# The third stage's order with a price on each change between gate products and RWKV's products, a shorter chunk pace, and a lower mark for gate products put in ahead

## The chip, the cores and the metric

The kernel runs on one core of one Trainium2 chip. The metric is the device time of one execution in microseconds (us); a lower time is better. One execution of the kernel before was profiled, and all rows below come from it. Names of engines are those of the profile: PE is TensorE (PEld its weight loads), DVE VectorE, ACT ScalarE, POOL GpSimd, SP the engine that issues the DMA transfers.

## What is computed

A trunk of two layers is applied to two sequences (1024 and 2048 tokens, width 1024). The first layer has an S5 mixer and a bidirectional RWKV-7 mixer, each multiplied by its own SiLU gate; the second is windowed attention. Cut to what matters for the change:

```
def s5_branch(u, z, p):
    ...
    y = jax.nn.gelu(y)
    y = y * jax.nn.sigmoid(y @ p['s5_glu_w'].astype(F32) + p['s5_glu_b'].astype(F32))
    return y * jax.nn.silu(z.astype(F32))

def rwkv_scan(r, w, k, v, kk, b, reverse):
    ...
    def step(S, inp):
        r_t, w_t, k_t, v_t, kk_t, b_t = inp
        sa = -jnp.einsum('bhvk,bhk->bhv', S, kk_t)
        S = (S * w_t[:, :, None, :] + sa[..., None] * b_t[:, :, None, :]
             + v_t[..., None] * k_t[:, :, None, :])
        return S, jnp.einsum('bhvk,bhk->bhv', S, r_t)
```

The RWKV state S goes through every token, once forward and once backward. The gates z and the S5 branch's GLU are plain matrix products with no order among the tokens.

## The kernel before

The kernel has four stages. The third (`mixers`) does two things at once on one core: RWKV's scan (`rwkv`), which is a long chain of small steps, and the gate work (`gates`), which is large and free of order. It takes the stretch from about 1114 to 2268 us of the profiled span.

**RWKV.** Tokens are cut into tiles of 128 and these into 4 chunks of 32. For each tile and direction: the decays (L1096, a scan on DVE at L1113), scaled keys on POOL (L1150, L1165), the inner products of a chunk (L1186 and L1187, masked on DVE at L1206), turned keys (L1196, copied by ACT at L1215), and for each window of four tiles the inverses of 32x32 triangular systems, 60 small DVE operations (L1251, L1253) between transposes. Then comes the chain proper, for each chunk: PE L1311, ACT L1314, PE L1320, ACT L1325, PE L1333 and L1334, DVE L1340, and the next chunk of that direction; the outputs (PE L1356, ACT L1363) hang off it. Both directions run side by side; there are 96 pairs of chunks (32 of the first sequence, 64 of the second).

**Gates.** 1536 products of 128x128 by 128x128 (L887, each two instructions in the trace) make z for both branches. When they are done, their weight tile `w` is used again for the GLU: 12 units of 256 tokens, each a load of S5's outputs, a gelu (ACT L932, DVE L934 and L936, ACT L938, DVE L940), 16 products of 128x256 (L970), and four times ACT L950, DVE L955 and a store. Two units' gelus are held at once (`act_at`), and two tiles of z (`zp`).

**What sets the order.** A planner (`Plan`) runs the tasks of both parts on a model of the engines, with a cost for each, and writes every engine's instructions in the order of the model's starts. On the chip each engine goes through its list in that order. Three numbers touch PE's list. A gate product has the last rank (`RF` is 9), so that it gets PE where it can start before the best RWKV task and end within `SLACK` of that start, and also ahead of an RWKV task that could start as early, where the columns of the model's last PE tasks would stay under `NEED`. `PACE` is the shortest distance in the model from one chunk of a direction to its next, in hundredths of a microsecond.

Of the kernel before, what the change touches and what calls it, by code (L numbers as in the profile page):

```python
# [34 lines left out]
class Event:  # L35


    def __init__(self, need=1, t=0.0):
        self.need, self.at = need, t
# [46 lines left out]
class Plan:  # L86
# [3 lines left out]


    SLACK = 0.25
    NEED = 3800
    ISSUE = 0.48
    AFTER = {"PE": 0.28, "SP": 0.0, "ACT": 0.1, "DVE": 0.14, "POOL": 0.1, None: 0.0}

    def __init__(self):
        self.clock = dict.fromkeys(self.AFTER, 0.0)
        self.queue = 0.0
        self.recent = deque()  # L100
        self.tasks = []
        self.now = 0.0

# [11 lines left out]
    def run(self):  # L115
        while self.tasks:
            best = {}
            for task in sorted(self.tasks, key=lambda x: x[0]):
                eng, cost, *waits = task[2]
                ts = [w if isinstance(w, float) else w.t for w in waits]  # L120
                if None in ts:
                    continue
                if eng == "SP":
                    n, cost = cost
                start = max(ts + [self.clock[eng] if eng else 0.0])
                if eng == "PE":
                    cost, cols = cost
                    if task[0] == 9 and eng in best and start <= best[eng][0] + 0.02:
                        end = start + best[eng][1]
                        if sum(c for t, c in self.recent if t > end - 3.413) + best[eng][2][2][1][1] < self.NEED:  # L130
                            best[eng] = start, cost, task
                            continue
                if eng not in best or (start < best[eng][0] and start + cost < best[eng][0] + self.SLACK):
                    best[eng] = start, cost, task
            assert best, "the plan is stuck"
            start, cost, task = min(best.values(), key=lambda x: x[0])
            eng = task[2][0]
            self.now = start
            if eng == "SP":
                n, cost = task[2][1]  # L140
                self.clock[eng] = start + self.ISSUE * n
                self.queue = max(self.queue + cost, start + self.ISSUE * n + 0.65 + cost / n)
                self.advance(task, self.queue + 1.1)
            else:
                if eng:
                    self.clock[eng] = start + cost
                if eng == "PE":
                    while self.recent and self.recent[0][0] < start - 4:
                        self.recent.popleft()
                    self.recent.append((start + cost, task[2][1][1]))  # L150
                self.advance(task, start + cost + self.AFTER[eng])

# [117 lines left out]
class Program:  # L270
# [5 lines left out]
    BACK = 2.0  # L276
    AFTER = {"PE": 0.2, "ACT": 0.14, "DVE": 0.13, "POOL": 0.08, "SP": 0.0}
    BEFORE = {"PE": 0.1, "ACT": 0.0, "DVE": 0.0, "POOL": 0.03, "SP": 0.1}
# [135 lines left out]
    def put(self):  # L414
# [17 lines left out]
        while done < len(ops):  # L432
# [27 lines left out]
            for j in after[i]:  # L460
                f = ops[j][0]
                early[j] = max(early[j], end + (0.0 if e == f == "PE" else self.AFTER[e] + self.BEFORE[f]))
                left[j] -= 1
# [7 lines left out]
class Kern:  # L471
# [3 lines left out]
    WIN = 2  # L475
    RM, RD, RC, RI = 2, 1, 1, 4
    GH = 2
    PACE, RF = 900, 9
    PACE2, LEFT = 600, 0
    GV = 2  # L480
    WR = "x", "mix"
# [545 lines left out]
    def rwkv(self, plan, st):  # L1027
# [59 lines left out]
        def decays():  # L1087

            for h in every:
# [21 lines left out]
                run = (lambda ap: ap[:, ::-1]) if d == 0 else (lambda ap: ap)  # L1111
                sx = lb.rearrange("c p n i -> c (p n i)")
                nc.vector.tensor_tensor_scan(run(sx), self.keep.rearrange("c n i -> c (n i)"), run(sx), 0.0, MULT, ADD)  # L1113
                t = yield "ACT", 0.66, t, ring_f1
                h["f1 free"] = ring_f1.take()
# [1030 lines left out]
```

## Time and profile before

| what | value |
|---|---|
| time, median of 3 runs | 4057.42 us (4056.36 to 4058.29) |
| time of the profiled execution | 4065.39 us |
| its span, from the first to the last instruction | 4063.7 us |
| mean granted TensorE clock in it | 0.97 |
| third stage in that span | about 1114 to 2268 us |

The profiled execution is 8.0 us over the median, and 1.7 us of its time lie outside its span. A difference that is worked out from its rows is added to the median.

### The profile page before, as it was taken

The page shows a single profiled execution, that of the slowest core. Times are in us where ns is not written, and L with a number is a line of the kernel's source. Part 1 is how long each engine was busy: PE and PEld are TensorE (multiplying, and loading weights), DVE is VectorE, ACT ScalarE, POOL GpSimd, SP SyncE. Part 2 cuts the span into 40 slices and gives each one's busy share as a digit, 9 for nine tenths or more (in the row PEclk, how much of TensorE's full clock was granted, in tenths as well). Part 3 has the DMA queues.
Part 4 walks back from the last instruction along what each step waited for, and adds up shares of the span by engine and source line. Part 5 has one row for each costly group of instructions (what it writes and reads, how often), then busy time and mean ns, then how long its engine had stood idle before and what let it go on. Part 6 is the DMA issues. An engine that isn't in the chain of part 4 may idle for free.

```text
span 4063.7 us, 87721 instructions
## 1 busy us (share of the span) xinstructions
PE 3763.6 (93%) x34128; PEld 3118.4 (77%) x34128; DVE 2821.8 (69%) x5545; ACT 1939.8 (48%) x4847; POOL 1615.8 (40%) x2007
## 2 busy tenths in 40 slices
PE   6878999999899999999998799999999999999999
PEld 4656766676688888878876577999999977778777
DVE  8356655666568878888887676544444469899997
ACT  3334333333345565555655322333323357777776
POOL 4422322232364555555540242222222335555554
PEclk9989999999999999999999899999999999999999
DMA  5677565566543334333344666644444422222221
GB/s 154 162 174 228 162 191 173 174 191 188 176 154 101 119 112 127 119 106 115 119 115 98 216 233 214 206 148 155 143 157 147 147 84 72 77 81 74 76 66 58
DMA packets 536324, 570.32 MB, mean 140 GB/s; under 512 B 93602, under 2 KB 436770, under 8 KB 525924
## 3 DMA queue, kind: packets, MB, share of 16 engines
q1 hardware_dynamic: 535908, 564.72, 45.4%
q8 instruction: 268, 4.39, 0.5%
q14 instruction: 148, 1.21, 0.1%
HBM read 398.03 MB, written 166.56 MB: 139 GB/s over the span
## 4 chain that ended last, share of the span: by engine, by line
PE 45%; DVE 17%; DMA 4%; issue 4%; POOL 3%; ACT 2%; SPq 1%; DVEq 0%; ACTq 0%; POOLq 0%
PE ps L412 30%; DVE sb L412 11%; PE acc L887 5%; PE pc L1333 2%; PE acc L970 2%; PE pg L1186 2%; ACT sb L412 2%; DMA rk<-rk 1%; DVE ng L1251 1%; DVE z L1253 1%; PE pY L1356 1%; PE pc L1320 1%; POOL lt L1165 1%; PE pc L1311 1%; DVE lt L1206 1%
## 5 line engine op out<-in xcount | busy, mean ns | idle before, releaser
L412 PE MATMUL ps<-sb 128*128 128x512 f32 (+8 forms) x12464 | 2542.2, 359 | 153.2 <-DVE sb L412 48.4
L412 PEld LDWEIGHTS ps<-sb 128*128 128x128 f32 (+2 forms) x12464 | 1958.8, 187 | 555.7 <-DVE sb L412 105.0
L412 POOL TENSOR_TENSOR sb<-sb,sb 128x384 f32<-128x384 f32 (+5 forms) x468 | 469.5, 1021 | 444.2 <-ACT sb L412 226.0
L412 POOL TENSOR_TENSOR sb<-sb 128x512 f32<-128x512 f32 (+5 forms) x358 | 320.7, 899 | 675.0 <-ACT sb L412 325.8
L412 DVE TENSOR_TENSOR sb<-ps,sb 128x512 fp32r<-128x512 f32 (+4 forms) x620 | 402.0, 661 | 189.7 <-PE ps L412 115.5
L412 POOL TENSOR_TENSOR sb<-sb,mhalf 128x8 f32<-128x8 f32 (+3 forms) x156 | 223.0, 1431 | 644.4 <-DVE sb L412 640.5
L887 PE MATMUL acc<-h,w 128*128 128x128 f32 x3072 | 448.0, 290 | 17.0 <-POOL rt L1280 14.3
L887 PEld LDWEIGHTS acc<-h,w 128*128 128x128 f32 x3072 | 383.1, 196 | 42.5 <-POOL rt L1280 14.5
L412 ACT ACTIVATE sb<-sb 128x256 fp32r<-128x256 f32 (+9 forms) x392 | 276.1, 710 | 286.3 <-DVE sb L412 128.5
L412 ACT COPY sb<-ps 128x512 f32<-128x512 f32 (+4 forms) x402 | 195.1, 502 | 438.0 <-PE ps L412 429.3
L412 PE MATMUL ps<-ident,sb 128*128 128x128 f32 x1888 | 317.2, 280 | 55.5 <-DVE sb L412 51.1
L412 DVE TENSOR_TENSOR sb<-sb,sb 128x256 fp32r<-128x256 f32 (+6 forms) x259 | 265.8, 1038 | 142.9 <-ACT sb L412 128.8
L412 ACT ACTIVATE sb<-sb,sb 128x384 f32<-128x384 f32 (+3 forms) x486 | 299.3, 619 | 111.5 <-DVE sb L412 60.4
L412 PEld LDWEIGHTS ps<-ident,sb 128*128 128x128 f32 x1888 | 237.6, 143 | 119.9 <-DVE sb L412 72.1
L1165 POOL TENSOR_TENSOR lt<-rk,lb 64x256 f32<-64x256 f32 x288 | 216.9, 761 | 196.3 <-PE pY L1356 84.8
L412 ACT ACTIVATE sb<-ps 128x512 f32<-128x512 f32 x108 | 64.5, 597 | 385.7 <-PE ps L412 385.7
L1325 ACT COPY rt<-pc 32x128 f32<-32x128 f32 x768 | 196.7, 256 | 97.7 <-PE pc L1320 86.6
L412 DVE CUSTOM_DVE_ANT_0 sb<-ps,sb,sb 128x384 f32<-128x384 f32 (+1 forms) x384 | 215.3, 588 | 28.6 <-PE ps L412 27.1
L1150 POOL TENSOR_TENSOR kb<-rk,f 128x128 f32<-128x128 f32 x384 | 197.6, 546 | 76.1 <-PE pg L1196 67.6
L412 ACT CAST sb<-ps 128x512 fp32r<-128x512 f32 x368 | 202.1, 587 | 50.9 <-PE ps L412 46.0
L1340 DVE TENSOR_TENSOR rt<-pc,wc 64x256 f32<-64x256 f32 x376 | 158.3, 421 | 71.5 <-PE pc L1334 36.1
L412 DVE TENSOR_SCALAR sb<-sb,sb 128x384 f32<-128x384 f32 (+4 forms) x264 | 190.6, 751 | 18.2 <-POOL sb L412 16.2
(121 smaller groups left out, 4680.1 us busy)
## 6 DMA issues: line engine op xcount, KB each, us to landing
sb<-wsp SPq DMA_DIRECT2D x65, 1024.0 KB
rk<-rk SPq DMA_DIRECT2D x96, 512.0 KB
sb<-in_od_w_in SPq DMA_DIRECT2D x36, 1024.0 KB
h<-h SPq DMA_DIRECT2D x48, 512.0 KB
sb<-in_od_w_z SPq DMA_DIRECT2D x24, 1024.0 KB
qkv<-sb SPq DMA_DIRECT2D x72, 256.0 KB
sb<-qkv SPq DMA_DIRECT2D x72, 256.0 KB
sb<-in_x_sample SPq DMA_DIRECT2D x32, 512.0 KB
```

The lines of the kernel that those rows point to most:

```text
L412: self.ops.append((eng, self.cost(eng, op, outs[-1] if outs[-1] is not k.get("accum_out") else outs[0], ins, a, k), deps, self.rank, lambd ...
L887: nc.tensor.matmul(sums[n][1][:, m * P:m * P + P], w[:, k, m * P:m * P + P], acts[n][0][:, k], start=k == 0, stop=k == KT - 1)
L970: nc.tensor.matmul(ps[:, 256 * (m % 2):256 * (m % 2) + 256], uw_at(k)[:, m], act_at(n)[:, 2 * k:2 * k + 2], start=k == 0, stop=k == 3)
L1150: nc.gpsimd.tensor_tensor(kb[:, sl, :, x, :], arr[n][:, sl, cs], f1[:, sl, cs, a:a + 32], MULT)
L1165: (nc.gpsimd if eng == "POOL" else nc.vector).tensor_tensor(ltv[:, :, :, at:at + 32], arr[n][rows, :, cs], f2[rows, :, cs, off:off + 32], ...
L1186: nc.tensor.matmul(g[64:P, c1, p], kb[0:64, p, c1].rearrange("c s i -> c (s i)"), lt[0:64, c1, 4 + p, 0:64], start=True, stop=True)
L1206: nc.vector.tensor_tensor(lt[rows, :, us, 0:64], g[rows], self.tri[h["d"]][rows].unsqueeze(1).unsqueeze(1).broadcast_to([64, 2, 4, 64]), MULT)
L1251: nc.vector.tensor_tensor(tv, z[:, 0:k, k:k + 1].broadcast_to([P, k, 31 - k]), z[:, k:k + 1, k + 1:32].broadcast_to([P, k, 31 - k]), MULT)
L1253: nc.vector.tensor_tensor(z[:, 0:k, k + 1:32], z[:, 0:k, k + 1:32], tv, ADD)
L1325: nc.scalar.copy(rt[rows, c1, 2 * q:2 * q + 2, :], pu[rows, 2:4])
L1333: nc.tensor.matmul(pu[0:64, 4 + p, :], lt[:, c1, 4 + p, 64:P], rt[:, c1, 4 + p, :], start=True, stop=True)
L1340: nc.vector.tensor_tensor(nrt[rows, n4 % 2, 4 - 4 * o:8 - 4 * o, :], pu[rows, 4:8], nh["wc"][rows, :, n4:n4 + 1].broadcast_to([64, 4, 64]) ...
```

## The change

The planner now adds a cost of 0.095 us to a PE task when the PE task before it was of the other sort (a gate product after an RWKV task, or the reverse). `PACE` goes from 900 to 800 and `NEED` from 3800 to 3000. No instruction is added or taken away; the five engines' lists hold the same work in another order. Lines after the new ones move down by up to 5 (L1311 becomes L1316).

```
-    NEED = 3800
+    NEED = 3000
     ISSUE = 0.48
+    TURN = 0.095
...
                 if eng == "PE":
                     cost, cols = cost
+
+                    cost += self.TURN * (self.wide != (task[0] == 9))
                     if task[0] == 9 and eng in best and start <= best[eng][0] + 0.02:
...
                 if eng == "PE":
+                    self.wide = task[0] == 9
...
-    PACE, RF = 900, 9
+    PACE, RF = 800, 9
```

How the order moves is shown at three places. The first is PE's list around the 145th and 146th chunk (counted over both directions), inside the second sequence. `acc` are gate products, `pc`, `pg` and `pY` RWKV's. Before:

```order
L887 MATMUL acc<-h,w 128x128 x2
L1096 MATMUL pg<-twt_6773,wup_6767 128x128 x4
L887 MATMUL acc<-h,w 128x128 x2
L1196 MATMUL pg<-ident,kb 128x128 x4
L887 MATMUL acc<-h,w 128x128 x3
L1311 MATMUL pc_20720<-rt_20380,lt_6777 32x64 x8
L887 MATMUL acc<-h,w 128x128 x13
L1320 MATMUL pc_20653<-u_20673,tt_20761 32x64 x8
L887 MATMUL acc<-h,w 128x128 x3
L1320 MATMUL pc_20720<-u_20738,tt_20782 32x64 x8
L887 MATMUL acc<-h,w 128x128 x2
```

The same chunks in the changed kernel's list on PE:

```order
L1316 MATMUL pc_20291<-rt_19968,lt_6847 32x64 x8
L1361 MATMUL pY<-rt_19704,lt_6837 32x64 x8
L1191 MATMUL pg<-lt_6832,kb 64x64
L1192 MATMUL pg<-lt_6832,kb 64x64
L1201 MATMUL pg<-ident,kb 128x128 x4
L892 MATMUL acc<-h,w 128x128 x6
L1101 MATMUL pg<-twt_6773,wup_6767 128x128 x4
L1191 MATMUL pg<-lt_6802,kb 64x64
L1192 MATMUL pg<-lt_6802,kb 64x64
L1316 MATMUL pc_20360<-rt_20004,lt_6777 32x64 x8
```

Six runs of gate products in eleven rows have become one in ten; the other products went to longer runs elsewhere.

The second place is the end of the stage on PE. Before, the last rows with units' products, among the last chunks:

```order
L1356 MATMUL pY<-rt_23551,lt_6797 32x64 x8
L970 MATMUL acc<-w 128x256
L1311 MATMUL pc_24022<-rt_23589,lt_6807 32x64 x8
L970 MATMUL acc<-w 128x256 x2
L1320 MATMUL pc_24022<-u_24032,tt_23399 32x64 x8
L970 MATMUL acc<-w 128x256 x3
```

The end of the stage on PE in the changed kernel, with the last chunk and what stands behind it:

```order
L1361 MATMUL pY<-rt_23300,lt_6842 32x64 x8
L975 MATMUL acc<-w 128x256
L1316 MATMUL pc_23729<-rt_23357,lt_6812 32x64 x8
L975 MATMUL acc<-w 128x256
L1325 MATMUL pc_23729<-u_23740,tt_22849 32x64 x8
L975 MATMUL acc<-w 128x256 x3
L1361 MATMUL pY<-rt_23357,lt_6812 32x64 x8
L975 MATMUL acc<-w 128x256 x176
```

176 of the 192 unit products (11 of 12 units) now stand behind the last RWKV product; before, none did.

The third place is ACT's list at the start of that new end (`w<-h` and `w<-w` are the gelu's two steps on ACT, `z` the units' outputs):

```order
L937 ACTIVATE w<-h 128x8x128
L955 ACTIVATE z<-acc,gb 128x256
L943 ACTIVATE w<-w 128x8x128
L955 ACTIVATE z<-acc,gb 128x256 x3
L937 ACTIVATE w<-h 128x8x128
L955 ACTIVATE z<-acc,gb 128x256 x2
```

The same steps stood before among RWKV's copies:

```order
L932 ACTIVATE w<-h 128x8x128
L1314 COPY u_22723<-pc_22702 128x128
L950 ACTIVATE z<-acc,gb 128x256
L1325 COPY rt_22057<-pc_22702 32x128 x4
L938 ACTIVATE w<-w 128x8x128
L1363 COPY ys_22351<-pY 128x128
```

The gelu's steps and the units' outputs have come to stand next to each other, with no RWKV work between them.

## Rows read from the trace of the kernel before

**Rows 1.** The page: span, and busy time of PE and DVE.
```profile
span 4063.7 us, 87721 instructions
...
PE 3763.6 (93%) x34128; PEld 3118.4 (77%) x34128; DVE 2821.8 (69%) x5545; ACT 1939.8 (48%) x4847; POOL 1615.8 (40%) x2007
```

**Rows 2.** Busy time by stretch of the third stage, with the granted clock.
```profile
core 0: us, PE busy (x) PEld busy (x) DVE busy (x) ACT busy (x) POOL busy (x), PEclk, DMA share, GB/s
1114.00:1314.00 200.00, 185.92 (x2691) 170.19 (x2695) 145.36 (x289) 92.80 (x266) 112.94 (x184) 0.96 0.41 133
1314.00:2083.00 769.00, 731.36 (x14248) 621.53 (x14239) 651.32 (x1358) 455.10 (x1472) 425.76 (x657) 0.98 0.39 118
2083.00:2268.00 185.00, 164.31 (x2605) 121.21 (x2600) 125.92 (x260) 103.15 (x302) 23.35 (x32) 0.94 0.40 91
```

**Rows 3.** Line L1311 in the first, second and third of these stretches.
```profile
L1311 PE MATMUL pc<-rt,lt x256: 216/219/260, 1143.4 to 1313.9; 128*32 128x64 f32 x128
...
L1311 PE MATMUL pc<-rt,lt x2296: 216/219/316, 1313.8 to 2075.5; 128*32 128x64 f32 x192
...
L1311 PE MATMUL pc<-rt,lt x528: 216/219/316, 2083.1 to 2265.1; 128*32 128x64 f32 x176
```

**Rows 4.** Timeline: one gate product (two instructions) between RWKV products; start, us.
```profile
1605.10 0.49 PE L887 MATMUL acc<-h,w 128*128 128x128 f32 x2
...
1605.52 0.43 PE L1320 MATMUL pc<-u,tt 32*32 32x64 f32 x16
...
1605.88 0.43 PE L1356 MATMUL pY<-rt,lt 128*32 128x64 f32 x16
```

**Rows 5.** Chain of waits, 1100 to 2290: runs of gate and of unit products.
```profile
1340.50 1.76 PE acc L887 x14
...
1478.36 1.98 PE acc L887 x16
...
2165.62 1.49 PE acc L970 x6
2170.49 1.92 PE acc L970 x8
```

**Rows 6.** DVE's waits, 1314 to 2083: us in total, times, longest.
```profile
DVE rt L1340 <- PE pc L1334: 18.5, 24, 1.7
DVE lt L1206 <- PE pg L1187: 16.0, 13, 2.7
...
DVE rt L1340 <- ACT rt L1325: 9.8, 3, 3.6
```

**Rows 7.** PE's longest wait, 1314 to 2083.
```profile
PE pg L1186 <- POOL lt L1165: 9.8, 8, 2.5
```

**Rows 8.** Timeline 2102 to 2122, ACT, then DVE: one gelu and unit outputs.
```profile
2103.92 1.05 ACT L932 ACTIVATE w<-h 128x1024 f32<-128x1024 f32 x1
...
2107.47 0.47 ACT L950 ACTIVATE z<-acc,gb 128x256 f32<-128x256 f32 x1 [1.72 <-issue]
2107.84 1.05 ACT L938 ACTIVATE w<-w 128x1024 f32<-128x1024 f32 x1
...
2105.01 0.69 DVE L934 TENSOR_SCALAR w<-w 128x1024 f32<-128x1024 f32 x1 [0.27 <-ACT w L932]
2105.74 1.23 DVE L936 TENSOR_TENSOR w<-w,h 128x1024 f32<-128x1024 f32 x1
2107.98 0.42 DVE L955 SCALAR_TENSOR_TENSOR z<-z,w 128x256 f32<-128x256 f32 x1 [1.01 <-ACT z L950]
2108.92 1.23 DVE L940 SCALAR_TENSOR_TENSOR w<-w,h 128x1024 f32<-128x1024 f32 x1 [0.52 <-ACT w L938]
```

**Rows 9.** Waits of ACT, then of PE, among the units, 2080 to 2268.
```profile
ACT z L950 <- DMA s<-z: 11.5, 7, 4.8
...
PE acc L970 <- ACT z L950: 5.3, 2, 4.9
```

More of the change, by code (lines that the diff above doesn't have):

```diff
@@ L100, in __init__ @@
         self.recent = deque()
+        self.wide = False
         self.tasks = []
```

## The prediction

> **What bounds the kernel now.** I read the page first: PE is busy for 93% of the span, DVE for 69% [rows 1], so PE looks like the bound everywhere. The change is in the third stage alone, so I cut that into stretches. A count of L1311 tells where the scan stands (16 instructions to a chunk, two chunks to a pair): 256 by 1314 us are 8 pairs, 2296 more by 2083 are 72 pairs, 528 by 2268 the last 16 [rows 3]. The middle stretch is the one to look at: 769 us for 72 pairs, 10.7 us a pair, PE busy for 731 us and DVE for 651 [rows 2]. These are two engines near their limit, not one. DVE's share there is 85%, and its waits say for whom it stops: 18.5 and 16.0 us for PE directly, 9.8 for an ACT copy that itself follows a PE product [rows 6]; some 44 us that a faster PE could give back. PE's own waits are shorter, the longest 9.8 us for POOL [rows 7]. The third view is the last stretch: 185 us for 16 pairs, in which all 12 GLU units run as well, and PE is busy for 164 [rows 2]; units and scan fill each other's gaps. The pace in the planner (9.0 us) is under what a pair takes, so the shorter one acts through the order that it gives, which I take from the changed lists.
>
> **The change part by part.** First the prices. A gate product inside a run costs PE 0.22 us (8 products take 1.98 us, 7 take 1.76 [rows 5]), but seven take 0.2 more than seven times that; a lone one holds PE for 0.42, from its start to the next RWKV product's [rows 4]. From RWKV product to RWKV product of another form the start moves on by 0.36 [rows 4], which a run in between doesn't shorten. So each run that ends before an RWKV product costs 0.19 us beyond its products. A unit's product costs 0.43 (1.92 less 1.49 for one product more [rows 5]).
>
> The Trainium skill's page "TensorE: Matmul & The Clock Gate" (section "Step-by-step: what each phase is for") says that PE pulls the next weight load ahead of matmuls in flight where row groups don't conflict or the background buffer is free, by which a change of sort would cost nothing. The rows show 0.19 us for each; by the rule the time below would be 4 us later, which lies inside the forecast's own range.
>
> Now I count products and runs in both lists (runs that end before a narrow RWKV product: 404 before, 279 now, besides those that end at wide ones, which cost nothing extra).
>
> First 8 pairs: 436 gate products become 372, 45 runs become 34: 64 x 0.224 + 11 x 0.19 = 16.5 us less for PE. PE was busy for 186 of these 200 us [rows 2], so I take all of it. Bounds: nothing (DVE, busy for 145 of 200, or the filling of the pipeline decides), and 16.5.
>
> Middle 72 pairs: 1100 gate products become 937, 293 runs become 186, 3 unit products go: 36.5 + 20.8 + 1.3 = 58.6 us less for PE. If PE alone were the bound, all of it would come. But DVE's work is the same (some 8 of the z operations leave), and 769 less 59 would ask 92% of it, where it did 85% [rows 2, 6]. What can come from DVE is what it now spends on waits that lead to PE, 44 us; each engine goes through a fixed list, and with PE early, the inversion's 60 operations stand in front of L1340 more often. I take half, 22 us. Bounds: 0 and 58.6.
>
> Last 16 pairs: 189 unit products (81.6 us) go out, 227 gate and 16 unit products (57.7 us) come in, runs fall from 66 to 58: 25.4 us less, and the 5.3 us that PE waits for a unit's output on ACT [rows 9] go with the units. I take 31 us; DVE, busy for 126 of 185 with the units' share in it [rows 2], is no bar. Bounds: 15 and 45, as PE's other 15 us of idleness stay, double or vanish.
>
> What stands behind: 176 unit products, 11 units, after the last chunk. This is new time, since nothing of RWKV is left to lie beside it. PE needs at least 176 x 0.43 = 76 us. But a unit waits for its gelu. The steps take 1.05, 0.69, 1.23, 1.05 and 1.23 us, and from the first start to the last end the trace has 6.2 us [rows 8]. The slot for unit n+2's gelu is free when unit n's last output has passed ACT and DVE (0.47 and 0.42 [rows 8]). Behind that comes the written order: DVE's second gelu step stands behind the first z of the unit that PE is at. That z is ready 3.45 (8 products) + 0.25 + 0.47 + 0.1 + 0.42 = 4.7 us after the unit's start, then follow L936, L938 and L940 with 1.23 + 1.05 + 1.23 and 0.4 for hops (the hop between L934 and L936 in [rows 8] is 0.04, the one from ACT to DVE 0.03 to 0.04, both rounded up). From one unit's start to the next's that is 8.65 us, where PE has work for 6.9. So 10 x 8.65 + 6.9 = 93.4, and some 2.5 us until the last output is on its way, where before an output of RWKV was: 96 us. Bounds: 76, and 114, where half of the units run their first half at the lower clock. The two z tiles and their stores also hold ACT (11.5 us in 7 waits [rows 9]), which speaks for the upper half.
>
> The 0.095 itself, the pace and the mark cost no instruction; POOL, SP and the loads of RWKV do the same work, and POOL (426 of 769 us busy [rows 2]) has room for it.
>
> **Sum.** -16.5 - 22 - 31 + 96 = +26.5 us. On the profiled execution's 4065.4 that is 4091.9, and on the median 4057.4 (8.0 lower) 4083.9.
>
> **The rivals.** One, faster: PE sets the pace after all, DVE keeps up, and the middle gives its 58.6 us; the units go at nearly PE's own rate, 80 us. Then -16.5 - 58.6 - 31 + 80 = -26, 4031 us. For it: PE's 95% in the middle against DVE's 85% [rows 2]. Against: DVE's waits for PE are 44 us, not 59 [rows 6]. With the tail at 96 it decides from a middle that is more than 48.5 us shorter.
>
> Two, no change: the middle gives 40 (nearly all that DVE waits for), the tail takes 88 (8 us a unit): -16.5 - 40 - 31 + 88 = 0, 4057 us.
>
> Three, much slower: the scan doesn't get ahead. The middle gives nothing, because DVE's list was made with inversions cheaper than they are and PE stands at L1186 and L1196 for masks, and PE's clock falls more often with fewer gate products to fill. It was at 0.98, 0.94 in the last stretch where PE was idle most [rows 2]; it has two levels, 1.2 and 2.4 GHz, so 0.98 is 4% of the time at the lower one. Twice that in the middle costs PE 15 us, the tail at 114 another 18: 4084 + 15 + 18 = 4117; without the clock 4106. I price it at 4110. The same page's Part 1 says that the clock is low by default and activity lifts it; the granted clock of the stretches agrees, and how far the changed order falls no run here shows.
>
> **How the numbers follow.** Chances: the forecast (4065 to 4100 as its own range) 0.47, faster 0.25 at 4031, no change 0.13 at 4057, much slower 0.15 at 4110. The range runs from 4026 to 4112: it leaves out the better third of the first rival and the worse half of the third. A measurement of this kernel tells some 0.2%, 8 us, from no change. Faster by more: 0.25 and a quarter of case two, 0.29; within: 0.12; slower: 0.59, the forecast and the third.
>
> **What would show it.** In the changed kernel's profile: the 8th pair at about 184 us after the stage's start; the middle at 735 to 755 us for 72 pairs with DVE's busy share at 87 to 89% and PE's below 95%; the last 16 pairs in about 155 us; then L970 (L975) alone for 90 to 105 us, in lots of 16 with gaps of about 1.7 us that end with DVE's L940 (L945). Wrong would be the middle at 715 or less, with DVE over 90%; a tail of 80 us without gaps; or a middle as long as before with PE waiting for DVE's L1206.

## The result, and the profile after

The changed kernel takes 4079.24 us (median of 4 runs, 4075.96 to 4080.89), the kernel before on the same chip 4056.89 us (4 runs, 4056.18 to 4058.29). The ratio is 1.0052, 95% interval 1.0037 to 1.0067: slower by 22 us, where 26.5 were forecast.

The page of the changed kernel answers to [rows 1]. PE is busy 15 us less than before in a span that is 15 us longer.

```profile
span 4078.5 us, 87788 instructions
...
PE 3748.5 (92%) x34128; PEld 3128.2 (77%) x34128; DVE 2815.7 (69%) x5545; ACT 1935.9 (47%) x4847; POOL 1595.3 (39%) x2007
```

Line L1316 tells where the scan stands, as L1311 does in [rows 3]: 2304 weight loads (72 pairs) between 1295 and 2040, and its last product at 2177. By these marks the stretches answer to [rows 2] so (columns as there; the fourth line is new, the units alone):

```profile
1114.00:1295.00 181.00, 167.82 (x2524) 154.58 (x2527) 136.71 (x276) 88.71 (x257) 105.17 (x181) 0.95 0.41 135
1295.00:2040.00 745.00, 681.75 (x13966) 585.51 (x13954) 645.07 (x1352) 446.39 (x1463) 412.94 (x659) 0.96 0.38 114
2040.00:2181.00 141.00, 132.14 (x2710) 111.75 (x2699) 88.48 (x205) 72.80 (x257) 25.13 (x36) 0.96 0.37 98
2181.00:2286.00 105.00, 83.12 (x350) 68.73 (x348) 46.79 (x75) 39.28 (x64) 0.00 (x0) 0.95 0.49 103
```

Read down the second column against [rows 2]: the first three stretches are 19, 24 and 44 us shorter, and 105 us stand behind them. What lies outside the stage is, taken together, within 2 us of before.

In the middle PE's waits answer to [rows 7] (us in total, times, longest):

```profile
PE pg L1191 <- POOL lt L1170: 13.1, 13, 3.3
PE pg L1191 <- DVE lt L1211: 9.8, 7, 2.6
PE pg L1192 <- DVE lt L1170: 8.7, 8, 1.5
PE pc L1316 <- DVE rt L1345: 5.8, 5, 2.7
```

and DVE's there to [rows 6]:

```profile
DVE lt L1211 <- PE pg L1192: 18.2, 12, 3.2
DVE rt L1345 <- PE pc L1339: 13.5, 15, 2.0
...
DVE rt L1345 <- ACT rt L1330: 8.5, 4, 3.0
DVE rt L1345 <- issue: 6.2, 5, 3.8
```

Summed over all rows of such views, before and after, PE's waits rise from 37 to 62 us, those of them that end with DVE from 14 to 33.

The tail's waits, all engines, 2181 to 2286, answer to [rows 9]:

```profile
DVE w L939 <- ACT w L937: 37.9, 10, 5.0
ACT w L937 <- DMA h<-ys: 30.6, 8, 4.3
...
PE acc L975 <- DVE w L945: 19.5, 9, 3.0
...
ACT z L955 <- DMA s<-z: 8.9, 11, 3.3
```

Behind each other they say that PE waits for the gelu's last step, DVE for its first, and that first step on ACT for the load of its input. The timeline from 2215 to 2236 shows one turn of it, PE first (start, us, then in brackets the idle time and its releaser):

```profile
2217.27 7.17 PE L975 MATMUL acc<-w 128*128 128x256 f32 x32 [1.11 <-DVE w L945]
2226.84 8.86 PE L975 MATMUL acc<-w 128*128 128x256 f32 x32 [2.39 <-DVE w L945]
```

SP's queue in the same stretch:

```profile
2215.60 2.69 SPq L933 DMA_DIRECT2D h<-ys  x4
2218.39 6.73 SPq L964 DMA_DIRECT2D s<-z  x4
2225.17 2.79 SPq L933 DMA_DIRECT2D h<-ys  x4
```

and the gelu's first step on ACT (L937), with the unit's outputs that stand behind it in ACT's list (L955), then DVE's part of both:

```profile
2221.18 1.06 ACT L937 ACTIVATE w<-h 128x1024 f32<-128x1024 f32 x1 [3.70 <-DMA h<-ys]
2222.15 0.82 ACT L955 ACTIVATE z<-acc,gb 128x256 f32<-128x256 f32 x2
...
2230.78 1.06 ACT L937 ACTIVATE w<-h 128x1024 f32<-128x1024 f32 x1 [3.75 <-DMA h<-ys]
```

```profile
2222.88 0.42 DVE L960 SCALAR_TENSOR_TENSOR z<-z,w 128x256 f32<-128x256 f32 x1
2223.22 1.22 DVE L941 TENSOR_TENSOR w<-w,h 128x1024 f32<-128x1024 f32 x1
2224.35 0.42 DVE L960 SCALAR_TENSOR_TENSOR z<-z,w 128x256 f32<-128x256 f32 x1
```

This is a loop from one gelu's L937 to the next one's. The two L955 stand behind L937 and wait for nothing but their turn, so PE had done their products. DVE's second L960 stands behind the gelu's second step (L941) and ends at 2224.77. SP then issues the second of the unit's four stores, and behind it, at 2225.17, the loads for the next gelu: 3.99 us after L937. From there to the next L937 it is 5.61 us (2230.78), so that a turn takes 9.6 us. The other turns in the middle of the tail take 9.5 to 10.2.

### The profile page after: what moved, and what is told of

Its sections match the earlier page's. It is cut to its first block, busy times and chain, and to the rows that moved or that the text cites. A ratio compares the mean times of both kernels' runs of the same rounds, so it can differ in the third digit from the quotient of the medians.

```text
span 4078.5 us, 87788 instructions
## 1 busy us (share of the span) xinstructions
PE 3748.5 (92%) x34128; PEld 3128.2 (77%) x34128; DVE 2815.7 (69%) x5545; ACT 1935.9 (47%) x4847; POOL 1595.3 (39%) x2007
## 4 chain that ended last, share of the span: by engine, by line
PE 37%; DVE 14%; ACT 3%; issue 3%; DMA 2%; SPq 1%; POOL 1%; DVEq 0%; ACTq 0%; POOLq 0%
PE ps L417 30%; DVE sb L417 10%; PE acc L892 2%; ACT sb L417 1%; PE pc L1338 1%; DVE ng L1256 1%; DVE z L1258 1%; PE acc L975 1%; DMA h<-ys 1%; DVE lt L1211 1%; DVE rt L1345 1%; PE pc L1325 1%; PE pg L1191 1%; PE pc L1316 1%; PE pY L1361 0%
## 5 line engine op out<-in xcount | busy, mean ns | idle before, releaser
L892 PE MATMUL acc<-h,w 128*128 128x128 f32 x3072 | 426.0, 288 | 17.5 <-POOL rt L1285 14.3
L1155 POOL TENSOR_TENSOR kb<-rk,f 128x128 f32<-128x128 f32 x384 | 181.9, 505 | 73.3 <-PE pg L1201 59.4
```

Of the source, the lines that this page charges most:

```text
L892: nc.tensor.matmul(sums[n][1][:, m * P:m * P + P], w[:, k, m * P:m * P + P], acts[n][0][:, k], start=k == 0, stop=k == KT - 1)
L1155: nc.gpsimd.tensor_tensor(kb[:, sl, :, x, :], arr[n][:, sl, cs], f1[:, sl, cs, a:a + 32], MULT)
```

## The experiments

The stretches below are read from each kernel's own profile by the same count. The kernel before was timed beside each group on the same chip, and the ratios are to that; on these chips it took 4068 to 4072 us. The profiles come from several chips, so that a few us between stretches are not read. "Low" is the time in the middle that the records of the granted clock put at the lower of its two levels (0.5 in the rows, 1.2 GHz).

| kernel | first | middle (low) | last | tail | ratio, 95% interval |
|---|---|---|---|---|---|
| before | 200 | 769 (34) | 185 | 0 | 1 |
| changed | 181 | 745 (65) | 140 | 104 | 1.0052, 1.0037 to 1.0067 |
| turn_alone | 195 | 766 (58) | 154 | 67 | 1.0095, 1.0075 to 1.0114 |
| need_alone | 201 | 791 (71) | 174 | 5 | 1.0046, 1.0030 to 1.0063 |
| pace_alone | 193 | 777 (51) | 174 | 0 | 0.9971, 0.9960 to 0.9982 |
| early_loads | 181 | 750 (68) | 141 | 110 | 1.0066, 1.0046 to 1.0086 |
| tail_z3 | 180 | 752 (82) | 141 | 102 | 1.0045, 1.0028 to 1.0062 |
| early_z3 | 181 | 742 (55) | 141 | 93 | 1.0013, 1.0000 to 1.0026 |
| inv_after | 173 | 716 (55) | 143 | 104 | one run, work left out |
| inv_before | 192 | 756 (34) | 185 | 0 | one run, work left out |
| nlt14 | 182 | 789 (58) | 177 | 9 | 1.0005, 0.9992 to 1.0019 |
| pace_turn05 | 187 | 797 (72) | 183 | 2 | 1.0043, 1.0026 to 1.0060 |
| turn05_nlt14 | 182 | 764 (31) | 176 | 0 | 0.9927, 0.9911 to 0.9944 |
| turn05_pace750_nlt14 | 180 | 779 (68) | 182 | 0 | 0.9971, 0.9959 to 0.9983 |

### One setting at a time

Each of the three kernels keeps one of the changed settings and takes the other two from before. The term for a turn alone:

```
-    NEED = 3000
+    NEED = 3800
-    PACE, RF = 800, 9
+    PACE, RF = 900, 9
```

> The price of 0.095 us for a change of sort alone, pace 900 and mark 3800 as before. By the counted order 117 unit products (7.3 units) come to stand behind the last RWKV product, and runs of gate products that end before a narrow product go from 404 to 396. Theory (units behind the scan are new time that the scan's gain doesn't pay): first stretch -8 us, middle -14, last 16 pairs -15, units alone +70: about +33 us, 4090. Rival (the price makes runs longer and PE saves 0.19 us for each, the loss in the changed kernel comes from the pace or the mark): -2 us, 4055.

Measured: 37.8 us over the kernel before (33 expected), with 117 unit products behind the scan in its order and a tail of 67 us. The term alone puts units behind the scan and costs more than all three settings together. The scan's gain came from other places than the theory had it: 4 us and not 14 in the middle, 31 and not 15 in the last pairs.

The lower mark alone:

```
-    TURN = 0.095
+    TURN = 0.0
-    PACE, RF = 800, 9
+    PACE, RF = 900, 9
```

> The mark 3000 alone, pace 900, no price. 40 runs fewer in the middle, 11 unit products behind the scan. Theory: 40 x 0.19 us with some 40% of it coming through, less some 4 us for the units behind: within 5 us of before, 4057. Rival (the mark keeps PE's clock up, so a lower one costs clock): granted clock in the middle under 0.97 and 4065 or more.

Measured: 19 us over. The rival held: PE's counted work in the middle falls by 7.6 us (253 runs in place of 293), and yet the middle is 22 us longer, with twice the time at the lower clock. The stretch's row, to compare with [rows 2]:

```profile
1314.40:2105.60 791.20, 737.68 (x14264) 627.59 (x14256) 648.03 (x1360) 455.67 (x1476) 415.49 (x657) 0.96 0.38 114
```

PE is busy for 6 us more than before with fewer runs: what the order saves in PE's work, the clock takes, as 37 us more at half speed cost up to 18. The other 16 of the 22 us are PE's idle time (38 to 54), so that the clock is not the whole loss.

The shorter pace alone:

```
-    NEED = 3000
+    NEED = 3800
-    TURN = 0.095
+    TURN = 0.0
```

> The pace 800 alone, mark 3800, no price. No unit product behind the scan, 374 runs for 404. Theory: 3 to 8 us faster, 4049 to 4054, and no stretch of units alone. Rival (the shorter pace packs the inversions so densely that the middle loses): the middle longer than 769 us and 4062 or more.

Measured: 9.8 us under the kernel before by the medians, a little more than the theory gave; the only one of the three settings that gains. The rival's longer middle came too (777 us); the gain lies in the first and the last pairs, 7 and 11 us.

### What bounds the tail

The gelu's inputs are loaded by a planner process of their own, so that they need not follow the earlier units' steps:

```
+        def early():
+            for n, (s, t0) in enumerate(units):
+                t = yield "SP", (4, 1.46), used["zs", 2 + n % 2], hr
...
+                inside[n].mark(t)
...
-                t = yield "ACT", 0.95, t, *([left[n - 2]] if n > 1 else [])
+                t = yield "ACT", 0.95, inside[n], *([left[n - 2]] if n > 1 else [])
...
+        plan.add(self.RG, early())
```

> The changed kernel with the loads of S5's outputs as a task of their own, so that they stand in SP's list two units ahead of their gelu; PE's list is the same in length. Theory now (in the stretch of units alone a gelu waits for its load, which stands on SP behind the outputs of the unit before; 8 waits of ACT with 30.6 us together in the changed kernel): 9.5 us a unit become 8.65, the stretch of 105 us becomes 95, the whole 10 us less than the changed kernel, 4069. Rival (the two z tiles and their stores, or PE, set the unit's time): the stretch stays at 103 to 107, 4079.

Measured: a tail of 110 us; the theory fell. Its waits show what took the load's place:

```profile
ACT z L964 <- DMA s<-z: 46.6, 16, 6.5
DVE z L969 <- ACT z L964: 45.4, 19, 6.6
```

ACT's unit output now waits for one of the two z tiles to be stored, 2.9 us each time. So the next pair of kernels has three z tiles, once with the loads as they were and once with the early ones:

```
-        zp = st.enter_context(tc.tile_pool(name="gz", bufs=2))
+        zp = st.enter_context(tc.tile_pool(name="gz", bufs=3))
...
-        hr, zr, ar = Ring(self.GH), Ring(2), Ring(2)
+        hr, zr, ar = Ring(self.GH), Ring(3), Ring(2)
```

> The changed kernel with three z tiles, the loads where they are. Theory (gelu loads stand behind the z stores on SP, and a store is issued when its z is ready, so a third tile moves the stores and with them the loads only by ACT's 9 us of waits in the tail): tail 98 to 104, the whole within 6 us of the changed kernel. Rival (the two z tiles alone set the unit's time): tail 85 to 95.

> The changed kernel with the gelu inputs loaded by a planner process of their own (as in early_loads) and with three z tiles in place of two. In early_loads ACT's z activation waited 46.6 us for z stores in the tail. Theory (what ends last in a unit is a transfer, first the load behind the stores, then the stores behind two z tiles): with both eased the unit falls from some 9.6 us to the 8.65 that ACT, DVE and PE's own links give, or less, the tail from 104 to 85 to 96 us, the whole 8 to 19 us under the changed kernel. Rival (the written order of DVE's second gelu step and PE's products set 9.6 us by themselves): the tail stays at 102 to 110 and the whole does not move.

Measured: 102 us with the tiles alone, 93 with both, which the theory gave. Neither edit alone takes anything worth having off the tail, both together take 11 us: two loops of nearly one length, through the loads and through the stores. Some 3 of the 11 us may be the clock's: PE is busy for 80.5 us there, against 83.1, at 0.98 in place of 0.95. The rest of that tail still has ACT waiting for stores; its row, then its waits:

```profile
2183.00:2276.00 93.00, 80.47 (x362) 67.70 (x354) 47.62 (x74) 38.93 (x65) 0.00 (x0) 0.98 0.51 112
```

```profile
ACT z L964 <- DMA s<-z: 32.3, 8, 5.0
...
PE acc L984 <- DVE w L954: 12.5, 7, 2.6
```

With the shorter tail the kernel is still no faster than before.

### What bounds the middle

In both orders the 60 small operations of the inversion on DVE, the multiplications and the additions, are cut to one column each; this leaves out part of the inverse. The additions:

```
...
-                    nc.vector.tensor_tensor(z[:, 0:k, k + 1:32], z[:, 0:k, k + 1:32], tv, ADD)
+                    nc.vector.tensor_tensor(z[:, 0:k, k + 1:k + 2], z[:, 0:k, k + 1:k + 2], tv[:, :, 0:1], ADD)
```

> The changed kernel with the 60 operations of the inversion on DVE cut to one column each; this leaves part of the inverse out, the order and the number of instructions on all engines stay. Theory (in the middle the engines wait for DVE, so that PE's saving of some 59 us could not all come): the middle falls from 745 us to 700 or less, PE's busy share there rises over 95%. Rival (PE with its clock and POOL set the middle): it stays at 735 or more.

> The kernel before with the same cut of the inversion's DVE operations, the order as it was. Theory (before, PE set most of the pace of the middle, and DVE added little): the middle falls from 769 us by at most 25, to 745 or more, less than in the changed kernel. Rival (DVE sets the pace in both alike): it falls by as much as in the changed kernel, 45 or more, to 725 or less.

The middle of the changed order with the cut:

```profile
1287.90:2004.30 716.40, 674.71 (x13954) 580.69 (x13946) 567.00 (x1351) 445.23 (x1463) 400.22 (x658) 0.96 0.40 118
```

and of the order before with it:

```profile
1312.70:2068.40 755.70, 728.83 (x14264) 619.85 (x14263) 575.78 (x1354) 454.81 (x1473) 407.29 (x657) 0.98 0.40 119
```

The changed order gives 28 us, less than the 45 expected and more than the rival's 10; PE's share is 94%, not over 95. The order before gives 14, as the theory had it. The difference between the orders grows from 25 to 39 us. So with DVE eased some 15 us more of PE's counted 58.6 come through. An estimated 4 of them are the clock's, as the changed order spends 10 us less at the lower level here (55 for 65) and each of these costs some 0.4 us (see the clock, below); DVE held back some 11 to 15. The waits say nearly the same: those of PE that end with DVE fall by 19 us in the changed order (33 to 14) and by 10 in the order before (14 to 4); those for POOL in the changed order stay (20 and 19).

### Toward a faster order

One left-factor tile fewer, the three settings as changed:

```
-    NLT = 15
+    NLT = 14
```

> The changed kernel, its three settings kept, with 14 left-factor tiles in place of 15. In the order that comes out all but 20 unit products lie inside the scan (first 8 pairs 379 gate products in 33 runs, middle 1151 in 197, last 16 pairs 172 unit products in 54 runs, behind the last chunk 20). Theory (the changed kernel loses by the units behind the scan and gains by PE's work taken out ahead of them): the first 8 pairs 15 to 18 us shorter than before, the middle 0 to 8 shorter (PE's sum is -8.1), the last 16 pairs 8 to 15 shorter, the tail 14 to 18, the whole 7 to 25 us under the kernel before. Rival (fewer columns asked for cost clock whatever the order, as in need_alone, and the tile that is missing makes PE wait for POOL): the middle at 775 or more, the whole at the time of before or over it.

Measured: no change; the tail is shorter than the theory's, but the whole gain is not there, and the rival's middle of 775 or more is. Its waits for POOL are not: PE waits 0.2 us for it there, and longest, 21.5 us, for nothing that the profile shows. Taking the units back into the scan won the tail; but the middle was 789 us, and the last pairs 177 in place of 140, since units stand among them again.

The term at about half, with 14 tiles:

```
-    TURN = 0.095
+    TURN = 0.05
...
-    NLT = 15
+    NLT = 14
```

> The changed kernel with the term for a turn at 0.05 in place of 0.095 and 14 left-factor tiles: nothing stands behind the last chunk (first 8 pairs 392 gate products in 37 runs, middle 1144 and 4 unit products in 214, last 188 in 63). By the prices of the prediction PE has -11.4 us in the first stretch, -4.7 in the middle and -1.0 in the last. Theory (these prices and no tail): 8 to 20 us under the kernel before. Rival (PE's saving is paid back by its clock and by waits for the left factors): no change or slower, with the middle at 775 or more.

Measured: 4039.40 us beside 4068.13, 29 us faster, more than the theory gave, and the best kernel of the study. In the last pairs PE's clock stays at 1.00, where it was 0.94 [rows 2]; no price had that. Its middle and its last pairs:

```profile
1304.00:2068.00 764.00, 714.74 (x14338) 618.62 (x14331) 645.26 (x1367) 451.42 (x1479) 429.54 (x657) 0.98 0.41 120
2068.00:2244.00 176.00, 158.11 (x2642) 116.98 (x2642) 133.09 (x276) 104.09 (x306) 32.25 (x41) 1.00 0.42 97
```

The mark at 3800 with the same term and 15 tiles:

```
-    NEED = 3000
+    NEED = 3800
-    TURN = 0.095
+    TURN = 0.05
```

> The pace of 800 as in the changed kernel, the term for a turn at 0.05, the floor on columns at 3800 as before, 15 left-factor tiles (first 8 pairs 398 gate products in 42 runs, middle 1138 and 4 unit products in 233, last 184 in 65, behind the scan 4). By the prices PE has -9.1 us in the first stretch, -2.4 in the middle, -2.3 in the last, and some 6 us come behind. Theory (pace alone gave 12 us, most of it where the PE sum is negative; the turn's term adds as long as it puts nothing behind the scan): 8 to 18 us under the kernel before, as fast as pace alone or faster. Rival (any term for the turn makes the planner stop filling and costs clock): the time of before or over it.

Measured: 17 us over the kernel before, by the ratio. The rival held, with the longest middle of all and 72 us of it at the lower clock, though the mark is the higher one: it is not the mark alone that sets how often the clock falls. Nor is it any term for a turn, as the rival had it: turn05_nlt14 has the same term and 31 us.

The best kernel with the pace at 750:

```
-    PACE, RF = 800, 9
+    PACE, RF = 750, 9
```

> The kernel with the term at 0.05, 14 left-factor tiles and a floor of 3000, and the pace at 750 in place of 800 (first 8 pairs 390 gate products in 33 runs, middle 1146 in 198, last 16 pairs 192 unit products in 56, nothing behind). By the prices PE has -12.6 us in the first stretch, -9.0 in the middle, -0.6 in the last: 5 us less than with 800. Theory (where nothing stands behind the scan the counted order ranks the kernels): 30 to 40 us under the kernel before, the middle at 755 to 765. Rival (the clock, which the count doesn't see, falls by the accident of the order: with 10 or more falls in the middle in place of 6 it is at 775 or more): no faster than 15 us under the kernel before.

Measured: 12.6 us under the kernel before, the rival again. PE has less counted work in the middle than with 800, and its stretch is 15 us longer:

```profile
1300.00:2080.00 780.00, 724.35 (x14364) 630.96 (x14360) 649.24 (x1361) 451.05 (x1472) 421.30 (x655) 0.96 0.40 117
```

The clock falls 17 times there, 6 times in the best kernel's middle, 7 in that of before, 14 in the changed one.

## Why the prediction was right, step by step

**The sum.** The terms were -16.5 - 22 - 31 + 96 = 26.5 us. The profiles give -18.5 - 24.6 - 44.4 + 104.0 = 16.5 for the stage and 14.9 for the two executions (4080.24 less 4065.39). The medians are 22.4 apart, since the profiled execution of before lay 8.5 over its median of these runs and that of the changed kernel 1.0. So every sign was right. That the total came within some 4 us is in part luck: two terms were off by 13 and by 8 the opposite way, and the rest came from which execution was profiled. Where its 8.5 us lay no run shows, so that up to as much of the three gains may not be the order's.

Some readings of the working were off by a little. The 2296 and 528 records in [rows 3] make 71.75 and 16.5 pairs, not 72 and 16: the boundary at 2083 lies 0.3 us too early. The runs of the three stretches now add up to 278, not 279, and at the 0.19 us that is stated the middle's terms give 58.1 and the first's 16.4; the loop's steps give 8.6.

**First 8 pairs.** The 8th pair stands 181 us after the stage's start (184 forecast). PE's busy time falls by 18.1, close to the counted 16.5, and all of it arrives.

**Middle.** The number held (745, within 735 to 755; DVE at 87%, PE at 92%), its reason only in part. It was right that PE's 58.6 us cannot all come because DVE is the second limit: the cut of the inversion shows some 11 to 15 us of it. It was wrong that the gain is what DVE had spent waiting for PE: those waits are 40 us still, against 44 [rows 6]. DVE's idle time falls by 18 us (118 to 100), and half of that lay in a row that the prediction didn't use, its waits for nothing shown ("issue"), which fall from 15.1 to 6.2 us. Before:

```profile
DVE rt L1340 <- issue: 15.1, 8, 4.3
```

And a part was not in the term but in the third rival: the clock. Time at the lower level went from 34 to 65 us, which at half speed costs PE up to 15. PE's busy time falls by 49.6 and not by 58.6, and its idle time rises by 26 (37.6 to 63.3). Of the 34 us that did not come, DVE's 11 to 15 and the clock's 12 to 15 leave some 4 to 11 that no run here explains.

A word on the price of a turn. PE's busy time in the middle is 49.6 us lower. Without a price on runs the count would give 37.8 us, less the 15 of the clock 23; with it 58.6 less 15, 44. The rows go with the price. So do two other orders: with turn05_nlt14 PE's busy time falls by 16.6 us, where its counted products alone would add 10 and its 79 fewer runs make that -4.7; with pace 750 it falls by 7.0, at +9 without the price and -9 with it, in spite of 34 us more at the lower clock. In both the fall is larger than the price makes it once the clock is counted, so that 0.19 us is rather too little.

The Trainium skill ("TensorE: Matmul & The Clock Gate", section "Step-by-step: what each phase is for") has the next weight load pulled ahead of the matmuls in flight under its conditions, by which a turn would be free; the trace does not agree for these turns, which cost the counted 0.19 us or more.

**Last 16 pairs.** The term was too small: -31 forecast, -44 measured. PE's busy time falls by 32.2: the counted 25.4 and half of the 13.4 us less at the lower clock (23.6 to 10.2), which was in no term. Its idle time falls from 20.7 to 8.9, 12 us and not the 5.3 of the one row that I took away: with gate products between the chunks, which wait for nothing, PE's other waits there shrink too.

**The tail.** 104 us, 8 more than forecast, and inside the bounds. The step that was off is the loop: I let the gelu wait for its slot and for DVE's place in the list (8.65 us a unit). DVE's place is a part of the loop, but the gelu waits for its input, which SP issues behind a store of an earlier unit (9.6 us), and no term had that wait. The forecast gap of 1.7 us on PE is 1.1 and 2.4 in the rows above, and it does end with DVE's L945; that link alone would have confirmed the wrong loop. Early loads and a third z tile together brought the tail to 93. That the forecast's loop came to 93.4 too does not confirm it, since ACT still waits for stores there.

**The rivals.** The faster case needed a middle over 48.5 us shorter, which no full kernel here had. The case of no change needed 40 us from the middle and a tail of 88; 25 and 104 came. The much slower case was right in its clock (twice the time at the lower level in the middle, priced at 15 us) and wrong in that the scan gains nothing. Its 4117 was also added up wrongly: it kept the 22 us of the middle that by its own words would not come, and with them gone it is 4139.

**The clock.** A fall in the changed kernel's middle, in windows (columns as above, the clock after POOL's):

```profile
1685.00:1688.60 3.60, 1.27 (x48) 1.04 (x48) 0.67 (x2) 2.36 (x9) 0.66 (x1) 1.00 0.86 282
1688.60:1693.00 4.40, 3.03 (x48) 2.55 (x48) 4.22 (x8) 1.16 (x5) 4.11 (x7) 0.50 0.03 11
```

and what PE waited for around it:

```profile
1686.33 0.27 PE L1338 MATMUL pc<-rt,lt 128*64 128x64 f32 x1 [1.60 <-ACT rt L1330]
...
1689.69 0.47 PE L1191 MATMUL pg<-lt,kb 64*64 64x64 f32 x2 [2.10 <-POOL lt L1170]
```

PE was busy for 1.27 of 3.6 us and had no gate product in hand for the gap; then the granted clock is at 0.5 (1.2 GHz) for 4.4 us. In a stretch as long as that of the first row, ahead of each of the 14 falls in this middle, start 1.6 instructions of gate products on the mean (two make a product), where the middle as a whole has 9.1 in as long a stretch. In the best kernel, with only 6 falls, it is 6.3 against 10.8, so that a lack of gate products doesn't mark every fall. The rows put the middle's length beside its time at the lower level (764 with 31, 769 with 34, then 777 to 797 with 51 to 72 where the gate products stay inside the scan). No run set the clock, but four of them share one order: changed, early_loads, tail_z3 and early_z3 have the same list on PE and on ACT in the middle (operations and tile names, in order), and their middles are 742 us with 55 at the lower level, 745 with 65, 750 with 68 and 752 with 82. The shortest and the longest:

```profile
1300.50:2042.20 741.70, 677.32 (x13954) 582.02 (x13946) 643.69 (x1351) 445.59 (x1463) 410.55 (x658) 0.96 0.38 114
1300.20:2052.50 752.30, 687.09 (x13954) 590.28 (x13946) 644.49 (x1352) 445.49 (x1463) 413.58 (x658) 0.95 0.38 113
```

That is 0.4 us for each us at the lower level, nearly all of it in PE's busy time. The twelve runs of nlt14, one program, say the same of the whole kernel: from 4060 us at a mean granted clock of 0.972 to 4085 at 0.964, 25 us for some 67 more at the lower level. By this price, an estimate, the 41 us that lie between the shortest and the longest middle of the other orders make about 16 of their 33 us. So the clock costs time in an unchanged order, and it is about half of what these orders differ by; the other half, and whether the gaps behind the falls cost time of their own, is open. Open too is why the order of turn05_nlt14 has so few falls; its neighbours, with one setting moved, have 13 (nlt14) and 17.

## What to carry to other kernels

Filler work beside a latency-bound chain fills the chain's gaps, but it must not be left over. A rule that makes the planner hold filler back moves it behind the chain, where it has loops of its own; count what stands behind the last link before counting what is saved inside. When two loops through different transfers have nearly one length, easing either shows nothing, so try both together before ruling one out. And a count of instructions ranks orders only as far as the gaps they leave are alike: two orders with 5 us between them by the count were 18 us apart the other way.

## What the runs showed that was not expected

Small moves of the planner's numbers change the middle by up to 33 us (764 to 797) with nearly the same counted work, and the time at the lower clock goes with it (31 to 72 us). That time differs between executions of one order, too: 55 to 82 us in the four that share the changed order's middle. The same kernel before took 4057 us in the first group and 4069, 4072, 4068 and 4070 in the later ones, with single runs from 4058 to 4083 in one of them; so only ratios within a group are compared.
